# Gate and up projections of a SwiGLU block with tokens on partitions: half-size products of 512 moving columns, turned for the down projection

## The chip, the core and the metric

The kernel runs on one core of one Trainium2 chip. A core has five engines with a queue each: TensorE (PE; its weight loads are listed as PEld), VectorE (DVE), ScalarE (ACT), GpSimd (POOL) and SyncE (SP, which here issues the loads and stores). The metric is the device time of one execution in microseconds, as a median over several runs. A profiled execution gives, beside its own time, a trace of every instruction; the span is the time from its first to its last instruction.

## The reference

One decoder block on 512 tokens of width 1024, all float32. Two token mixers (retention and forgetting attention) are merged and projected, and a gated feed-forward follows, which is what the change touches:

```python
h2 = rmsnorm(x, g_ffn[l])
ff = (jax.nn.silu(h2 @ w_gate[l]) * (h2 @ w_up[l])) @ w_down[l]
x = x + ff
```

`x` is (512, 1024), `w_gate` and `w_up` are (1024, 2816), `w_down` is (2816, 1024). The norm is one factor per token (`rstd`) and one weight per column (`g_ffn`).

## The kernel before

**Numbers in two parts.** Every float32 operand of a large product is split into a high part in the type float32r (a cast on ACT) and a low part, the difference (a subtraction on DVE). Each 128-deep step of a product is then three matmuls: high by high, and the two mixed ones (`three`). A weight therefore costs a load, a cast on ACT and a subtraction on DVE before PE can use it.

**Half-size products.** A product of two matrices cut into 2x2 blocks is formed from seven block products instead of eight, with sums of blocks on both sides (Strassen's scheme in Winograd's form). The sums of x are called S1 to S4, the sums of weights T1 to T4. `xfh` and `xfl` hold the parts of x, feature-major, one pair of tiles for each of four pairs of column blocks j, in slots A11, A21, A12, A22, S1, S2, S3 of 256 tokens; S4 takes A21's slot when that is no longer needed. x carries `g_ffn` already; the factor per token, `r2`, is applied to the results. It is `rstd2` spread over all partitions: `broadcast_cols` copies it wide, turns it on PE and copies it back.

**Gate and up.** Results lie with features on partitions, in `pf`, 22 tiles of 128 features by 512 tokens. The first 256 features of gate and of up are whole products of 512 moving columns (`whole_products`, 48 matmuls each). The other ten blocks of 256 features, gate and up in turn, are half-size products (`half_products`): the weight block is the stationary operand, x the moving one, with 256 tokens per matmul, 7 products x 4 steps x 3 = 84 matmuls. Their weights come one block ahead through `factors`: one load of 1 MB, three DVE operations of sums and three pairs of cast and low part, in tiles of 1024 and 1536 columns. `quarters` adds the pieces up on DVE, then the gate is multiplied by r2 and goes through silu, and up is multiplied in.

**Down.** The last 14 of the 22 tiles of `pf` go through whole products (`prepare` loads and splits a row block of `w_down` and splits pf's tile; eight accumulators, one for each 128 output columns, fill all eight banks of PSUM; tiles `hl` hold pf's parts). During that stage `p_sums` makes the sums for the first eight tiles, which go through half-size products with weights from `factors` and end in the store.

**Order.** PE's order is the program's wherever `pinned` is set. On DVE and ACT a scheduler orders the instructions when the program is built, except where `after(a, b)` puts a behind b. `queue(ins)` does that for DVE: each instruction given to it comes behind the one given before. The first stages of the kernel (values and gate of the retention, "v/g stage" below) already hold tokens on partitions and use `queue`, for instance with `sum_half` (L407) and `split_raw` (L154, L155). Tiles of one tag share a place in memory; a new tile waits until the old one has been read. Names in the trace leave out the number of a buffer, and every matmul is recorded at L72, every turn (a 128x128 transpose against the identity matrix) at L75.

Of the kernel before, what the change touches and what calls it, by code (L numbers as in the profile page):

```python
# [17 lines left out]
P = 128  # L18
D = 1024
# [34 lines left out]
def block_kernel(ctx: ExitStack, tc, x, xT, c_early, c_tab, c_late, w_qf, w_tok, w_vg, w_a, w_y, w_o, w_gu, w_dn, w_dh, out):  # L54
# [812 lines left out]
    r2 = xp.tile([P, S], F32, name="r2")  # L867
# [45 lines left out]

    B12, B11, B21, B22 = range(4)
    wpools = [wq]
    WT = {"raw": (4, F32), "t13": (2, F32), "t24": (2, F32), "ah": (3, F32R), "al": (3, F32R),
# [3 lines left out]
    def wtile(tag):  # L920
        n, dt = WT[tag]
        two = tag in ("raw", "ah", "al") and len(wpools) > 1
        i = seen.get(tag, 0)
        seen[tag] = i + 1
        return wpools[i % 2 if two else 0].tile([P, n, 512], dt, name=tag, tag=tag)
# [22 lines left out]
    def blocks_of(src, n):  # L948

        raws = [wtile("raw")] if n == 0 else [wtile("t13"), wtile("t24")]  # L950
        for v, raw in enumerate(raws):
            nc.sync.dma_start(out=raw, in_=src if n == 0 else src[:, 2 * v:2 * v + 2, :])
        h, l, ah, al = (wtile(t) for t in (f"ch{n}", f"cl{n}", "ah", "al"))
        cuts = ((raws[0], slice(0, 1), h, l, slice(0, 1)),)
        cuts += ((raws[0], slice(1, 4), ah, al, slice(0, 3)),) if n == 0 else ((raws[0], slice(1, 2), ah, al, slice(0, 1)), (raws[1], slice(0, 2), ah, al, slice(1, 3)))
        for raw, a, hh, ll, b in cuts:
            blocks_of.last = nc.scalar.copy(out=hh[:, b, :], in_=raw[:, a, :]), tt(out=ll[:, b, :], in0=raw[:, a, :], in1=f32(hh)[:, b, :], op=ALU.subtract)
        return {"B12": ((h, l), 0), "B11": ((ah, al), 0), "B21": ((ah, al), 1), "B22": ((ah, al), 2)}

    def whole_products(w, ks, step):  # L960
        accs = [bank("acc") for _ in range(2)]
        for n, k in enumerate(ks):
            j, odd = k // 2, k % 2
            mh, ml = (f[j][:, 2 * odd:2 * odd + 2, :].rearrange("p s t -> p (s t)") for f in (xfh, xfl))
            for m2 in range(2):
                (h, l), i = w[f"B{odd + 1}{m2 + 1}"]
                fs = slice(j * P, (j + 1) * P)
                three(accs[m2], h[:, i, fs], l[:, i, fs], mh, ml, n == 0, n == NK - 1)
            step(n)
        return accs  # L970

# [8 lines left out]
    def half_products(w, q, casts=None):  # L980

        x, y, z = (bank(t)[:, 0:HT] for t in ("sc", "acc", "acc"))
        u = fp.tile([P, 4, HT], F32, name="u", tag="u", bufs=2)
# [20 lines left out]


    ws = [blocks_of(w_gu[0, 0], 0)]
    x_sums(3)
    tmp.release()
    mgp.release()
    wp.release()  # L1010
    fp = tc.alloc_tile_pool(name="fp", bufs=1, side="left")
    fp.tile([P, 64], F32, name="pad")
    wpools += [fp]
    pf = fp.tile([P, NF, S], F32, name="pf")
    r2b = r2.rearrange("p (o t) -> p o t", o=1).broadcast_to([P, 2, S])
    rstd2 = rstd1
    EVEN_FIRST = (0, 2, 4, 6, 1, 3, 5, 7)

    def beside_gate(n):
        if n == 6:  # L1020
            pb = bank("tp")
            for t in range(NT):
                mm(pb[:, t:t + 1], lhsT=sqs[:, t * P:(t + 1) * P], rhs=ones[:, 0:1], start=True, stop=True)
            rsqrt(rstd2, pb[:, 0:NT], 1.0 / D, [P, NT], "n1", behind=blocks_of.last[1])

    def beside_up(n):
        if n == 6:
            broadcast_cols(rstd2, r2, fp.tile([P, 4, HT], F32, name="d", tag="d")[:, 0:2, :].rearrange("p a (b t) -> p (a b) t", t=P))
            for m2 in range(2):
                tt(out=pf[:, m2, :], in0=gate[m2], in1=r2, op=ALU.mult)  # L1030
# [231 lines left out]
```

## Time and profile before

| what | value |
|---|---|
| median of 3 runs | 707.72 us (707.56 to 708.82) |
| the profiled execution | 709.25 us, its span 707.5 us |
| granted TensorE clock, mean | 0.999 |
| PE busy | 701.2 us (99% of the span) |
| DVE busy | 535.5 us (76%) |
| ACT busy | 362.0 us (51%) |
| first gate matmul to first matmul of the whole down products | 360.87 to 587.62 us, 226.75 us |
| whole down products | 587.62 to 663.80 us, 76.18 us |
| half-size down products and the end | 663.80 to 707.50 us, 43.70 us |

The profiled execution lies 1.5 us above the median. In the lines shown below, a row of a timeline gives start, length, engine, line of the program, operation, output <- inputs, shapes, and, in brackets, the engine's idle time before it with what ended it. A row of the groups gives the count, the busy time and the mean ns of one. A recorded matmul is longer than the distance to the next, since matmuls overlap; the pace is read from the starts.

### The profile page before, as it was taken

What the parts mean: (1) busy time and instruction counts of PE and PEld (TensorE: products, weight loads), DVE (VectorE), ACT (ScalarE), POOL (GpSimd) and SP (SyncE); (2) the same over time, 40 slices, a digit from 0 to 9 for tenths busy, and PEclk for the clock granted to TensorE, in tenths of its full rate; (3) what the DMA queues carried; (4) which work ended last, traced back from release to release, by engine and by line L of the source; (5) the groups of instructions that cost most, each with busy time, mean ns of one, the idle gap of its engine ahead of it and who ended that gap; (6) DMA issues with size and microseconds to landing.
All of it is one profiled execution on the core that took longest, in us unless ns stands there. A gap on an engine that the chain in (4) does not pass through costs nothing.

```text
span 707.5 us, 10876 instructions
## 1 busy us (share of the span) xinstructions
PE 701.2 (99%) x4283; PEld 619.2 (88%) x4283; DVE 535.5 (76%) x873; ACT 362.0 (51%) x558; POOL 71.6 (10%) x90
## 2 busy tenths in 40 slices
PE   8999999999999999999999999999999999999998
PEld 6888988888877768888888999999999998888998
DVE  6799477754788765748867989898988997844694
ACT  6677453232667566326544755565566555433251
POOL 0004941201122110000220000000000000000000
PEclk9999999999999999999999999999999999999999
DMA  7901312223432312239212322332233114343112
GB/s 280 419 20 31 120 60 90 75 84 99 132 106 91 103 61 65 93 111 327 89 32 88 121 87 93 120 120 71 110 120 120 60 61 134 117 166 113 51 62 74
DMA packets 20547, 77.37 MB, mean 109 GB/s; under 512 B 2440, under 2 KB 3080, under 8 KB 17296
## 3 DMA queue, kind: packets, MB, share of 16 engines
q1 hardware_dynamic: 20352, 76.67, 32.1%
q8 instruction: 33, 0.54, 0.3%
q14 instruction: 18, 0.15, 0.1%
q10 hardware_dynamic: 144, 0.02, 0.0%
HBM read 73.52 MB, written 2.11 MB: 107 GB/s over the span
## 4 chain that ended last, share of the span: by engine, by line
PE 95%; DVE 2%; DMA 1%; issue 1%; ACT 1%; POOL 0%; SPq 0%; DVEq 0%; POOLq 0%
PE acc L72 60%; PE sc L72 28%; PE tp L72 5%; PE tp L75 2%; DMA raw<-in_w_tok_dram 1%; POOL cb L680 0%; DMA cb<-cd 0%; DVE tq L667 0%; DVE pr L688 0%; DVE sg L737 0%; ACT tk L659 0%; DVE pr L692 0%; ACT pr L690 0%; ACT wh L154 0%; DVE ri L691 0%
## 5 line engine op out<-in xcount | busy, mean ns | idle before, releaser
L154 ACT CAST wh<-raw 128x1024 fp32r<-128x1024 f32 (+1 forms) x44 | 46.1, 1049 | 83.4 <-PE acc L72 79.4
L72 PE MATMUL sc<-xfh,cl 128*128 128x256 f32 x288 | 83.2, 289 | 0.0
L72 PE MATMUL sc<-xfh,ch 128*128 128x256 f32 x288 | 81.6, 283 | 0.0
L72 PE MATMUL sc<-xfl,ch 128*128 128x256 f32 x288 | 81.4, 283 | 0.0
L155 DVE TENSOR_TENSOR wl<-raw,wh 128x1024 fp32r<-128x1024 f32 (+1 forms) x44 | 57.0, 1296 | 17.7 <-ACT wh L154 17.5
L929 DVE TENSOR_TENSOR cl<-t,ch 128x1024 fp32r<-128x1024 f32 x48 | 58.6, 1222 | 13.7 <-ACT ch L929 13.6
L72 PE MATMUL acc<-xfh,ah 128*128 128x256 f32 (+1 forms) x216 | 63.9, 296 | 0.0
L72 PE MATMUL acc<-xfh,al 128*128 128x256 f32 (+1 forms) x216 | 63.7, 295 | 0.0
L72 PE MATMUL acc<-xfl,ah 128*128 128x256 f32 (+1 forms) x216 | 63.7, 295 | 0.0
L929 ACT CAST ch<-t 128x1024 fp32r<-128x1024 f32 x48 | 50.5, 1052 | 12.8 <-PE tp L72 8.0
L72 PEld LDWEIGHTS sc<-xfh,cl 128*128 128x128 f32 x288 | 55.0, 191 | 0.8 <-DVE cl L929 0.2
L72 PEld LDWEIGHTS sc<-xfh,ch 128*128 128x128 f32 x288 | 55.1, 191 | 0.2
L72 PEld LDWEIGHTS sc<-xfl,ch 128*128 128x128 f32 x288 | 55.1, 191 | 0.0
L72 PE MATMUL acc<-xh,wh 128*128 128x512 f32 x128 | 53.2, 416 | 0.0
L72 PE MATMUL acc<-wh,xh 128*128 128x512 f32 (+2 forms) x144 | 50.4, 350 | 0.0
L72 PE MATMUL acc<-xh,wl 128*128 128x512 f32 x128 | 50.2, 392 | 0.0
L72 PE MATMUL acc<-xl,wh 128*128 128x512 f32 x128 | 50.0, 391 | 0.0
L72 PE MATMUL acc<-wh,xl 128*128 128x512 f32 (+2 forms) x144 | 49.4, 343 | 0.0
L72 PE MATMUL acc<-wl,xh 128*128 128x512 f32 (+2 forms) x144 | 49.3, 342 | 0.0
L929 DVE TENSOR_TENSOR al<-raw,ah 128x1536 fp32r<-128x1536 f32 x24 | 42.2, 1756 | 6.9 <-ACT ah L929 6.9
L72 PEld LDWEIGHTS acc<-xfh,al 128*128 128x128 f32 x216 | 41.3, 191 | 1.0
L72 PEld LDWEIGHTS acc<-xfl,ah 128*128 128x128 f32 x216 | 41.3, 191 | 0.9
(322 smaller groups left out, 1903.2 us busy)
## 6 DMA issues: line engine op xcount, KB each, us to landing
raw<-in_w_gu_dram SPq DMA_DIRECT2D x21, 1024.0 KB, 4.8
raw<-in_w_a_dram SPq DMA_DIRECT2D x16, 512.0 KB, 3.6
t<-in_w_dn_dram SPq DMA_DIRECT2D x14, 512.0 KB, 3.6
blk<-in_w_vg_dram SPq DMA_DIRECT2D x8, 512.0 KB, 10.0
raw<-in_w_tok_dram SPq DMA_DIRECT2D x8, 512.0 KB, 3.6
raw<-in_w_y_dram SPq DMA_DIRECT2D x8, 512.0 KB, 3.6
raw<-in_w_o_dram SPq DMA_DIRECT2D x8, 512.0 KB, 3.9
raw<-in_w_dh_dram SPq DMA_DIRECT2D x4, 1024.0 KB, 5.0
```

What stands on the lines that cost most here:

```text
L72: in_order(nc.tensor.matmul(o, **kw))
L75: in_order(nc.tensor.transpose(out=o, in_=src, identity=ident))
L154: split_raw.last = (nc.scalar.copy(out=h[:, :width], in_=raw[:, :width]), tt(out=l[:, :width], in0=raw[:, :width], in1=f32(h)[:, :width], ...
L155: tt(out=l[:, :width], in0=raw[:, :width], in1=f32(h)[:, :width], op=ALU.subtract))
L929: split_to.last = nc.scalar.copy(out=h, in_=src), tt(out=l, in0=src, in1=f32(h), op=ALU.subtract)
```

## The change

Gate and up are computed with tokens on partitions. Now x is the stationary operand and the weights move, and the 2x2 blocks of the weights are no longer halves of one matrix: the two column halves are gate and up. The 2816 features go in six groups, five of 512 and one of 256 (`GROUPS`); in each group a block product has 4 steps (j) x 2 halves of 128 tokens (tp) x 3 matmuls of 512 (256) moving columns, seven of them (`gu`): A12, A11, S1, S2, S3, S4, A22, in this order.

A group's weights come as eight loads of 512 KB (`load_group`), into tiles of their own. The sums of weights are made in place (`sum_of`), half a block at a time (two of the four j), and each half is split by `part` into one of three places (`ring_parts`). Every sum and every low part goes through `queue`, in the order written.

Results are collected in `us` (two tiles, one for each tp), copied from PSUM by ACT (`keep`) and added up on DVE through `queue`. The factor per token is now a scalar per partition, so it goes into silu's scale and into the final multiplication; r2, its broadcast and the multiplications by it are gone. `put_h` turns the result on PE, four 128x128 transposes for each of 22 chunks of 128 features, and ACT copies each chunk into `pf`. For group g this happens during group g + 1, and for the last group behind the first matmuls of the down stage.

The whole down products keep their count; their tiles lie in other places, their first matmuls are reordered, and `prepare` and `p_sums` no longer multiply by r2. The pool `wq` is released behind them, and a new pool `wd` holds the tiles of the half-size down products in its place; `factors` for the first of these is called behind the whole products instead of ahead of the last of them.

```diff
-def block_kernel(ctx: ExitStack, tc, x, xT, ..., w_o, w_gu, w_dn, w_dh, out):
+def block_kernel(ctx: ExitStack, tc, x, xT, ..., w_o, w_gu, w_gl, w_dn, w_dh, out):
...
+    GROUPS = [512] * 5 + [256]
+    ring, fq = [0], None
+    def load_group(g, which):
+        w = GROUPS[g]
+        for b in which:
+            if b == B21 and g % 2:
+                halves_ = fq.tile([P, 2, 1024], F32, name="b21", tag="b21")
+                halves_ = [halves_[:, v, :] for v in range(2)]
+            else:
+                halves_ = [wq.tile([P, 1024], F32, name=f"b{b}{v}", tag=f"b{b}{v}") for v in range(2)]
+            for v in range(2):
+                nc.sync.dma_start(out=halves_[v][:, :2 * w], in_=w_gu[g, b, v] if w == 512 else w_gl[b, v])
+            raws[g][b] = [f[:, :2 * w] for f in halves_]
+    def ring_parts():
+        i = ring[0] % 3
+        ring[0] += 1
+        if i < 2:
+            return [wq.tile([P, 1024], F32R, name=n, tag=f"{n}{i}") for n in ("ph", "pl")]
+        hl = fq.tile([P, 2, 1024], F32R, name="hl", tag="hl")
+        return [hl[:, v, :] for v in range(2)]
+    def part(raw, pinned_=True):
+        w2 = raw.shape[-1]
+        h, l = (f[:, :w2] for f in ring_parts())
+        nc.scalar.copy(out=h, in_=raw)
+        low = tt(out=l, in0=raw, in1=f32(h), op=ALU.subtract)
+        if pinned_:
+            queue(low)
+        else:
+            turn_of[0] = low
+        return h, l
+    def sum_of(g, b, c, v):
+        queue(tt(out=raws[g][b][v], in0=raws[g][b][v], in1=raws[g][c][v], op=ALU.add))
+        return raws[g][b][v]
+    def gu(os, parts, slot, new, w, by_bank=False, middle=None):
+        steps = [(j, tp) for j in range(4) for tp in range(2)]
+        for i, (j, tp) in enumerate(sorted(steps, key=lambda s: s[1]) if by_bank else steps):
+            if i == 4 and middle:
+                middle()
+            h, l = parts[j // 2]
+            cs = slice(j % 2 * w, j % 2 * w + w)
+            sh, sl = (f[j][:, slot, tp * P:(tp + 1) * P] for f in (xfh, xfl))
+            for n, (a, b) in enumerate(((sh, h), (sl, h), (sh, l))):
+                mm(os[tp][:, :w], lhsT=a, rhs=b[:, cs], start=new and j + n == 0, stop=j == 3 and n == 2, skip_group_check=not new)
+    HALF = 8
+    parts_of = {}
+    def prepare(k):
+        n = k - HALF
+        raw = wq.tile([P, 1024], F32, name="raw", tag=("b00", "b01", "b30", "b31")[n % 4])
+        nc.sync.dma_start(out=raw, in_=w_dn[n])
+        h, l = ring_parts()
+        cast = nc.scalar.copy(out=h, in_=raw)
+        if n > 0:
+            after(cast, prepare.last)
+        tt(out=l, in0=raw, in1=f32(h), op=ALU.subtract)
+        if n % 4 == 0:
+            hl = xp.tile([P, 2, S], F32R, name="hl", tag="s4")
+        elif n % 4 == 3:
+            hl = fq.tile([P, 2, S], F32R, name="hl", tag="b21")
+        else:
+            hl = wq.tile([P, 2, S], F32R, name="hl", tag=f"b2{n % 4 - 1}")
+        ph, pl = hl[:, 0, :], hl[:, 1, :]
+        prepare.last = nc.scalar.copy(out=ph, in_=pf[:, k, :])
+        if n > 0:
+            after(prepare.last, cast)
+        tt(out=pl, in0=pf[:, k, :], in1=f32(ph), op=ALU.subtract)
+        parts_of[k] = (h, l, ph, pl)
...
+    raws = [[None] * 4 for _ in GROUPS]
+    load_group(0, (B11, B12, B21, B22))
+    ahead = {0: [part(raws[0][B11][0], False), part(raws[0][B11][1])]}
+    for v in range(2):
+        sum_of(0, B11, B12, v)
+    x_sums(3)
+    tmp.release()
+    mgp.release()
+    wp.release()
+    fq = tc.alloc_tile_pool(name="fq", bufs=1, side="left")
+    fq.tile([P, 64], F32, name="pad")
+    second = [part(raws[0][B21][v]) for v in range(2)]
+    rstd2 = rstd1
+    fp = None
+    hs = {}
+    def put_h(g, cs):
+        for c in cs:
+            pb = bank("tp")
+            for t in range(NT):
+                turn(pb[:, t * P:(t + 1) * P], hs[g][t][:, c * P:(c + 1) * P])
+            nc.scalar.copy(out=pf[:, 4 * g + c, :], in_=pb)
+    pinned[0] = True
+    for g, w in enumerate(GROUPS):
+        us = [fq.tile([P, 4, 512], F32, name=f"us{tp}", tag=f"us{tp}") for tp in range(2)]
+        us = [f[:, :, :w] for f in us]
+        x_, z_, y_ = [bank("acc") for _ in range(2)], [bank("acc") for _ in range(2)], [bank("sc") for _ in range(2)]
+        def keep(slot, os):
+            for tp in range(2):
+                nc.scalar.copy(out=us[tp][:, slot, :], in_=os[tp][:, :w])
+        if g == 0:
+            gu(x_, ahead[0], A11, True, w)
+            keep(0, x_)
+            gu(y_, second, A12, True, w)
+            parts = [part(raws[0][B11][v]) for v in range(2)]
+            for j in range(4):
+                split_x(j, S4, s4[:, j, :])
+            fp = tc.alloc_tile_pool(name="fp", bufs=1, side="left")
+            pf = fp.tile([P, NF, S], F32, name="pf")
+        else:
+            gu(y_, ahead[g], A12, True, w)
+            put_h(g - 1, (0, 1))
+            second = [ahead[g, 1], part(raws[g][B11][1])]
+            gu(x_, second, A11, True, w, middle=lambda: put_h(g - 1, (2, 3)))
+            keep(0, x_)
+            parts = [part(sum_of(g, B11, B12, v)) for v in range(2)]
+        if g + 1 < len(GROUPS):
+            load_group(g + 1, (B21,))
+        gu(z_, parts, S1, True, w)
+        keep(3, z_)
+        if g == 0:
+            pb = bank("tp")
+            for t in range(NT):
+                mm(pb[:, t:t + 1], lhsT=sqs[:, t * P:(t + 1) * P], rhs=ones[:, 0:1], start=True, stop=True)
+        parts = [part(sum_of(g, B11, B22, v)) for v in range(2)]
+        gu(x_, parts, S2, False, w)
+        keep(1, x_)
+        if g == 0:
+            turn_of[0] = rsqrt(rstd2, pb[:, 0:NT], 1.0 / D, [P, NT], "n1", behind=turn_of[0])
+        for tp in range(2):
+            queue(tt(out=us[tp][:, 0, :], in0=y_[tp][:, :w], in1=us[tp][:, 0, :], op=ALU.add))
+            act(out=us[tp][:, 0, :], in_=us[tp][:, 0, :], func=AF.Silu, scale=rstd2[:, tp:tp + 1])
+        parts = [part(sum_of(g, B12, B22, v)) for v in range(2)]
+        if g + 1 < len(GROUPS):
+            load_group(g + 1, (B12,))
+        gu(x_, parts, S3, False, w)
+        keep(2, x_)
+        parts = [part(raws[g][B22][v]) for v in range(2)]
+        if g + 1 < len(GROUPS):
+            load_group(g + 1, (B22,))
+        gu(z_, parts, S4, False, w)
+        parts = [part(sum_of(g, B11, B21, v)) for v in range(2)]
+        if g + 1 < len(GROUPS):
+            load_group(g + 1, (B11,))
+        for tp in range(2):
+            queue(tt(out=us[tp][:, 3, :], in0=us[tp][:, 3, :], in1=us[tp][:, 2, :], op=ALU.subtract))
+        if g + 1 < len(GROUPS):
+            ahead[g + 1] = [part(raws[g + 1][B21][0])]
+        gu(x_, parts, A22, False, w, by_bank=True)
+        for tp in range(2):
+            queue(tt(out=us[tp][:, 1, :], in0=z_[tp][:, :w], in1=us[tp][:, 1, :], op=ALU.subtract))
+        for tp in range(2):
+            queue(stt(out=us[tp][:, 0, :], in0=us[tp][:, 1, :], scalar=rstd2[:, tp:tp + 1], in1=us[tp][:, 0, :], op0=ALU.mult, op1=ALU.mult))
+        if g + 1 < len(GROUPS):
+            ahead[g + 1].append(part(raws[g + 1][B21][1]))
+        else:
+            prepare(HALF)
+        for tp in range(2):
+            act(out=us[tp][:, 2, :], in_=x_[tp][:, :w], func=AF.Silu, scale=rstd2[:, tp + 2:tp + 3])
+            queue(stt(out=us[tp][:, 2, :], in0=us[tp][:, 3, :], scalar=rstd2[:, tp + 2:tp + 3], in1=us[tp][:, 2, :], op0=ALU.mult, op1=ALU.mult))
+            if tp == 0 and g + 1 < len(GROUPS):
+                ahead[g + 1, 1] = part(raws[g + 1][B11][0])
+        hs[g] = [us[0][:, 0, :], us[1][:, 0, :], us[0][:, 2, :], us[1][:, 2, :]]
+    pinned[0] = False
+
+    accs = [bank(("sc", "acc", "acc", "tp")[b // 2]) for b in range(8)]
+    x1q = x1.rearrange("p (g a) (s t) -> p g (a s) t", a=2, s=2)
+    pinned[0] = True
+    def whole(k, ms):
+        h, l, ph, pl = parts_of[k]
+        for m in ms:
+            fs = slice(m * P, (m + 1) * P)
+            three(accs[m], h[:, fs], l[:, fs], ph, pl, k == HALF, k == NF - 1)
+            if k == NF - 1:
+                tt(out=x1[:, m, :], in0=accs[m], in1=x1[:, m, :], op=ALU.add)
+    whole(HALF, (0, 1, 4, 5, 2, 3))
+    put_h(len(GROUPS) - 1, (0, 1))
+    prepare(HALF + 1)
+    whole(HALF + 1, (0, 1, 4, 5, 2, 3))
+    whole(HALF, (6, 7))
+    whole(HALF + 1, (6, 7))
+    for k in range(HALF + 2, NF):
+        prepare(k)
+        if (k - HALF) % 3 == 2 and k // 3 - 3 < 4:
+            p_sums(k // 3 - 3)
+        whole(k, range(NK))
+    wq.release()
+    wd = tc.alloc_tile_pool(name="wd", bufs=1, side="right")
+    WT = {"raw": (4, F32, "us0"), "ah": (3, F32R, "b21"), "al": (3, F32R, "hl"), "t13": (2, F32), "t24": (2, F32),
...
-    def whole_products(w, ks, step):
...
-    r2b = r2.rearrange("p (o t) -> p o t", o=1).broadcast_to([P, 2, S])
...
-    for n in range(2, NF):
-        f2, g = n // 2, n % 2
-        if n < NF - 1:
-            ws.append(factors(w_gu[(n + 1) % 2, (n + 1) // 2]))
-        else:
-            prepare(HALF)
-        pp = pf[:, 2 * f2:2 * f2 + 2, :]
-        qq = pp.rearrange("p a (s t) -> p (a s) t", s=2)
-        q = qq if g == 0 else fp.tile([P, 4, HT], F32, name="d", tag="d")
-        done = half_products(ws[n], q, factors.casts if n < NF - 1 else None)
-        if n == 2:
-            after(factors.casts[0], half_products.early)
-            for m2 in range(2):
-                after(act(out=pf[:, m2, :], in_=pf[:, m2, :], func=AF.Silu), half_products.early)
-                tt(out=pf[:, m2, :], in0=up[m2], in1=pf[:, m2, :], op=ALU.mult)
-        quarters(q, *done)
-        if g == 0:
-            tt(out=pp, in0=pp, in1=r2b, op=ALU.mult)
-            act(out=pp, in_=pp, func=AF.Silu)
-        else:
-            tt(out=qq, in0=qq, in1=q, op=ALU.mult)
...
-    for k in range(HALF, NF):
-        if k > HALF:
-            prepare(k)
-        if (k - HALF) % 3 == 2 and k // 3 - 3 < 4:
-            p_sums(k // 3 - 3)
-        if k == NF - 1:
-            ws = [factors(w_dh[0])]
-        h, l, ph, pl = parts[k]
...
+    u2 = fq.tile([P, 2, 4, HT], F32, name="u2", tag="us1")
+    def u_tile():
+        turns_u[0] += 1
+        return u2[:, turns_u[0] % 2]
+    turns_u = [0]
+    ws = [factors(w_dh[0])]
```

More of the change, by code (lines that the diff above doesn't have):

```diff
@@ L53, in block_kernel @@
 @with_exitstack
[L54 removed]
+def block_kernel(ctx: ExitStack, tc, x, xT, c_early, c_tab, c_late, w_qf, w_tok, w_vg, w_a, w_y, w_o, w_gu, w_gl, w_dn, w_dh, out):
     nc = tc.nc
@@ L1026, in beside_up @@
[L1026 to L1030, printed above, removed]
-        if n < 4:
-            split_x(n, S4, s4[:, n, :])
-    pinned[0] = True
-    ws.append(blocks_of(w_gu[1, 0], 1))
-    gate = whole_products(ws[0], (0, 2, 4, 1, 3, 5, 6, 7), beside_gate)
-    seen["raw"] = 2
```

115 lines of the change are left out of this document (23 added, 92 removed).

## The prediction

> **What bounds the kernel now.** I read the page first: total, busy engines, clock, chain of waits, DMA issues.
>
> ```profile
> span 707.5 us, 10876 instructions
> PE 701.2 (99%) x4283; PEld 619.2 (88%) x4283; DVE 535.5 (76%) x873; ACT 362.0 (51%) x558; POOL 71.6 (10%) x90
> PEclk9999999999999999999999999999999999999999
> PE 95%; DVE 2%; DMA 1%; issue 1%; ACT 1%; POOL 0%; SPq 0%; DVEq 0%; POOLq 0%
> t<-in_w_dn_dram SPq DMA_DIRECT2D x14, 512.0 KB, 3.6
> raw<-in_w_dh_dram SPq DMA_DIRECT2D x4, 1024.0 KB, 5.0
> ```
>
> TensorE (PE) holds 95% of the chain at full clock. Second, the table by stage, cut at the first gate matmul, the first of the whole down products, and the first half-size down product.
>
> ```profile
> core 0: us, PE busy (x) PEld busy (x) DVE busy (x) ACT busy (x) POOL busy (x), PEclk, DMA share, GB/s
> 360.87:587.62 226.75, 226.73 (x1790) 221.98 (x1789) 200.11 (x257) 125.67 (x188) 2.64 (x2) 1.00 0.28 96
> 587.62:663.80 76.18, 76.18 (x338) 63.06 (x338) 50.21 (x57) 31.15 (x35) 0.00 (x0) 1.00 0.37 118
> 663.80:707.50 43.70, 40.55 (x337) 40.24 (x335) 29.51 (x40) 15.16 (x24) 0.00 (x0) 0.99 0.20 73
> ```
>
> Gate and up last 226.75 with PE never idle; VectorE (DVE) is second at 200, ScalarE (ACT) at 126. Third, the chain in order of time (start, length, what).
>
> ```profile
> 30.13 16.32 PE acc L72 x72
> ...
> 403.05 2.88 PE sc L72 x24
> 405.93 1.44 PE acc L72 x12
> ...
> 413.21 2.88 PE sc L72 x24
> ```
>
> 72 matmuls of 512 columns in 16.32: 0.2267 each. 12 of 256 columns in 1.44: 0.1200. A block of 256 features (84 matmuls) recurs every 413.21 - 403.05 = 10.16, so 512 features of gate and up cost 40.6.
>
> **The change: PE.** Before: 1680 matmuls of 256 columns and 96 of 512. After: five groups of 168 with 512 columns (38.1 each) and one of 168 with 256 (20.2): 210.6. Added are 88 turns of 128x128. From the timeline of PE:
>
> ```profile
> 74.52 0.60 PE L75 MATMUL tp<-ctab,wide 128*128 128x128 f32 x4
> 74.96 0.60 PE L75 MATMUL tp<-ctab,rot 128*128 128x128 f32 x4
> 75.32 0.36 PE L72 MATMUL acc<-wh,xh 128*128 128x256 f32 x1
> 75.52 0.28 PE L72 MATMUL acc<-wl,xh 128*128 128x256 f32 x1
> ```
>
> Eight turns take 75.32 - 74.52 = 0.80, and the matmul behind them 0.20 instead of 0.12: 0.88 a pair of chunks. Ten of the eleven pairs fall in this stage (8.8), one in the down stage (0.9). With the 0.8 of the column sums of squares, which stay, PE needs 210.6 + 8.8 + 0.8 = 220.2 against 226.75: 6.5 less; 5.6 with the eleventh pair. The removed broadcast of r2 is inside the 226.75.
>
> The Trainium skill speaks against this gain: "TensorE: Matmul & The Clock Gate", section "Back-to-back issue gap", gives columns / 2.4 + 2.5 ns per matmul. By it a merged pair saves 2.5 ns, not the 13.3 of the rows; 840 pairs give 2.1, the 6144 fewer columns 2.6, and the turns would eat both: an estimate of some 231 for PE alone. The rows are of this kernel's own matmuls, so they decide.
>
> **VectorE's chain.** A weight half (two of the four column pairs, 128x1024) must be cast to its high part by ACT, and DVE must subtract that to get the low part; for S1, S2, S3 and A22 DVE first adds two blocks. New is that `queue` strings DVE in the order written: sum 0, low 0, sum 1, low 1. The low part waits for ACT's cast, the cast for that sum, and DVE, which takes its queue in order, stands still meanwhile; behind it stand the next sum and, through that, the next product. The same pattern runs in this kernel's v/g stage. DVE there:
>
> ```profile
> 36.91 1.23 DVE L407 TENSOR_TENSOR blk<-blk,blk 128x1024 f32<-128x1024 f32 x1
> ...
> 40.45 0.16 DVE L115 TENSOR_SCALAR n1v<-ss 128x4 f32<-128x4 f32 x1
> ...
> 42.74 1.23 DVE L155 TENSOR_TENSOR wl<-blk,wh 128x1024 fp32r<-128x1024 f32 x1
> ...
> 47.37 1.22 DVE L407 TENSOR_TENSOR blk<-blk,blk 128x1024 f32<-128x1024 f32 x1
> 48.51 1.22 DVE L419 TENSOR_TENSOR sl<-sums,sh 128x1024 fp32r<-128x1024 f32 x1
> 49.76 1.23 DVE L155 TENSOR_TENSOR wl<-blk,wh 128x1024 fp32r<-128x1024 f32 x1
> 50.91 1.22 DVE L407 TENSOR_TENSOR blk<-blk,blk 128x1024 f32<-128x1024 f32 x1
> ...
> 62.56 1.28 DVE L460 TENSOR_TENSOR vr<-sc,u 128x512 f32<-128x512 f32 x2
> 63.76 1.61 DVE L155 TENSOR_TENSOR wl<-raw,wh 128x1024 fp32r<-128x1024 f32 x1
> ```
>
> and ACT beside it:
>
> ```profile
> 38.22 1.06 ACT L154 CAST wh<-blk 128x1024 fp32r<-128x1024 f32 x1 [0.69 <-DVE blk L407]
> 40.37 0.59 ACT L429 COPY u<-acc 128x512 f32<-128x512 f32 x1 [1.09 <-PE acc L72]
> 40.87 1.05 ACT L154 CAST wh<-blk 128x1024 fp32r<-128x1024 f32 x1
> ...
> 48.68 1.06 ACT L154 CAST wh<-blk 128x1024 fp32r<-128x1024 f32 x1 [0.57 <-DVE blk L407]
> ```
>
> Sum at 47.37, cast from 48.68 to 49.74, low part at 49.76, next sum at 50.91: one link is 3.54, and so is 36.91 to 40.45. In the v/g stage another operation fills the wait (48.51); in the new loop none stands between. A half on PE is 12 x 0.2267 = 2.72, so a product made of sums is fed slower than it is eaten. Per group of 512, eight halves are sums, six are not (low part 1.14, from 49.76 to 50.91), and ten operations of 512 elements take 0.60 each (two from 62.56 to 63.76): 8 x 3.54 + 6 x 1.14 + 10 x 0.60 = 41.2. That exceeds PE's 38.1 + 1.76 = 39.8: DVE's chain becomes the bound, idle ten us of each 41 while it sets the pace.
>
> Where it shows: call 0 the start of product A12. B11's second half can be cast only when its place in the ring of three is read (2.7 + 0.2), and with what DVE still owes the last group the first sum of S1 starts near 5.5. Six links (21.2), the two additions to us0 (1.2) and some 0.3 for ACT copies ahead of a cast bring S3's last low part to 28.2 to 28.6. PE wants it after 5.4 + 0.9 + 5.4 + 0.9 + 5.4 + 5.4 + 2.7 + 0.45 = 26.6. So S3 stalls about 1.9, and a group takes 41.7. Behind S3 the chain recovers: S4's halves need no sum, and A22 goes bank by bank, so its second half is wanted only after a quarter of the product. Were S3's delay gone, the 41.2 of the chain would still bind, and the wait would come up at A22 or at the next S1. A ring place that is freed late shifts the same wait about and adds little to it.
>
> The first group needs no S1 sums on the way, but `rsqrt` stands in the chain (40.45 to 42.74, 2.3): PE 38.9, late 2.6, so 41.5. For the last, half as wide, durations by form, DVE and then ACT:
>
> ```profile
> L943 DVE TENSOR_TENSOR t<-t,raw 128x512 f32<-128x512 f32 x19 | 13.1, 688 | 0.4
> L1003 DVE TENSOR_TENSOR d<-u 128x256 f32<-128x256 f32 x10 | 4.2, 425 | 6.6 <-ACT u L993 6.6
> ```
>
> ```profile
> L929 ACT CAST ch<-t 128x1024 fp32r<-128x1024 f32 x38 | 40.0, 1053 | 1.5 <-issue 1.5
> L1091 ACT ACTIVATE pf<-pf 128x512 f32<-128x512 f32 x2 | 1.2, 626 | 0.0
> L1059 ACT CAST hl<-pf 128x512 fp32r<-128x512 f32 x1 | 0.6, 620 | 1.0 <-DVE pf L1058 1.0
> L252 ACT COPY r<-tp 128x512 f32<-128x512 f32 x1 | 0.6, 587 | 3.4 <-PE tp L75 3.4
> ```
>
> A link is 0.69 + 0.62 + 0.60 + 0.08 = 1.99; 8 x 1.99 + 4 x 0.60 + 10 x 0.37 = 22.0, as much as PE (20.2 + 1.8); with a stall at S3 as above, 23.5. Stage: 41.5 + 4 x 41.7 + 23.5 = 231.8, **5.0 more** than 226.75.
>
> What I cost at nothing: ACT's 14 casts, 8 copies, 4 silu and 4 copies of turned chunks (14.7 + 4.7 + 2.5 + 2.3 = 24 per 41), hidden as long as none stands ahead of a cast (rival B). The loads: 4 MB a group as before, in 512 KB pieces; B11's next half is asked for behind A22's sum and lands 3.6 later, under A22's 5.4; uncovered it would cost up to 3.6 a group. SP's queue only holds loads. GpSimd has nothing here. The start: the fourth column pair of x is first wanted 4.1 after 360.87, and its low part is there:
>
> ```profile
> 361.87 0.75 DVE L902 SCALAR_TENSOR_TENSOR xfl<-x,ce,xfh 128x512 fp32r<-128x512 f32 x1
> ```
>
> In the down stage `prepare` loses its multiplication by r2 and `p_sums` gains splits: DVE has 26 free of 76.
>
> **Two seams.** First, k = 8: its weights take the ring place that S4 of the last group frees 2.9 before PE needs them; cast 1.05, two low parts 1.9, among six short DVE operations. Between 0.3 and 2.5; I take 1.4, since the short ones (0.4 each) may come ahead. The accumulators wait for nothing longer: the first four columns of output use banks that are read early. Second, the half-size down products. Before, their first weights came early:
>
> ```profile
> 647.30 1.48 ACT L929 CAST ah<-raw 128x1536 fp32r<-128x1536 f32 x1 [3.87 <-PE tp L72]
> ```
>
> ```profile
> 648.81 1.76 DVE L929 TENSOR_TENSOR al<-raw,ah 128x1536 fp32r<-128x1536 f32 x1 [2.71 <-ACT ah L929]
> ```
>
> that is 16 ahead of 663.80. Now pool `wd` lies where `wq` lay, and k = 21 reads wq's ring and b20 to its last matmul. If `ah` falls on these, cast and low part follow the end: 1.5 + 1.8 + 0.2 = 3.5. Nothing if it falls elsewhere; 8.2 if even the load (5.0) must wait. I take 2.5.
>
> Sum: 5.0 + 0.9 + 1.4 + 2.5 = 9.8 on the span of 707.5. That execution took 709.25, 1.5 above the median 707.72 of the runs, so I add the difference to the median: **717.5**.
>
> **Rivals.**
> A, faster: the chain does not bind and the seams are hidden: 707.72 - 5.6 = 702.1. A link would have to be under (39.8 - 6.8 - 6.0) / 8 = 3.37; the two links seen are 3.54, so the margin is only 5%. For it the Trainium skill, "Perfetto Trace Analysis", section "Identifying the Most-Contended Engine", judges TensorE by the busy share of weight loads: it is 98% here, and the change drops two loads in five. The trace disagrees that loads set the pace: at 83% (63.06 of 76.18) a matmul still pays the same 13 ns.
> B, much slower: on ACT a PSUM copy (`keep`) is queued ahead of the next product's cast, as at 40.37, where a copy waited 1.09 for PE with a cast behind it. The cast then follows the product's end: 0.2 + 1.1 + 1.05 + 1.22 - 0.45 = 3.1 of PE wait. One such place a group gives five times 3, near 732.5; four would pass 770.
> C, a wash: links as seen, but lateness only just over and the seams hidden, within 0.2% (1.4 us, about what a measurement of this kernel tells from no change).
>
> **Numbers.** DVE's chain with its seams 0.59 (711 to 724: stage 2 to 9 over, as a link takes 3.44 to 3.65 and copies cost up to one more us a group, and the seams' own ends), B 0.16, A 0.16, C 0.09. Slower is the first and B, 0.75; same 0.09; faster 0.16. The range 704 to 733 leaves out the better half of A and the part of B with more than one such place a group, together about 0.18.
>
> **What would show it.** After: some 41.7 between the A12 starts of groups; DVE idle behind ACT casts, about 1.1 at each low part of a sum; PE waiting at S3 for DVE; pairs of turns at 0.88; PE idle near 2.5 before the first half-size down product. Wrong if PE runs through the groups at 39.8 (A), if ACT's idle time before `keep` copies is ended by PE with casts behind (B), or if 512-column matmuls come at another pace than 0.2267.

## The result: slower, by twice what was forecast

The changed kernel takes 729.92 us (median of 4 runs, 729.45 to 732.05) against 708.27 of the kernel before in the same session (4 runs, 707.56 to 708.89): a ratio of 1.0312, 95% interval 1.0288 to 1.0336. The forecast was 717.5.

### The profile after

From the page of the changed kernel: the span, TensorE's share, the granted clock by slices and the chain that ended last.

```profile
span 728.3 us, 9535 instructions
PE 707.4 (97%) x3599; PEld 587.7 (81%) x3599; DVE 520.0 (71%) x845; ACT 373.0 (51%) x570; POOL 72.2 (10%) x90
...
PEclk9999999999999999999999999999999999999799
...
PE 80%; DVE 9%; ACT 6%; issue 3%; DMA 2%; POOL 1%; ACTq 0%; SPq 0%; DVEq 0%; POOLq 0%
```

TensorE is busy for longer than before (707.4 against 701.2) although it has less to do. Part of its waiting is counted as busy: a matmul that comes behind a wait is recorded longer (0.50 instead of 0.39 at 428.30), and the four middle groups show 163.94 busy where a later version, in which TensorE does not stand still, needs 159.60. The chain shows it better: TensorE holds 80% of it, before 95%. The clock drops in one slice, from 674 to 692 us.

The table by stage, cut at the starts of the first group, the second group, the last group, the whole down products and the half-size down products (columns as in the table of before):

```profile
360.74:404.39 43.65, 41.30 (x177) 33.12 (x176) 34.82 (x48) 26.45 (x35) 3.16 (x2) 0.96 0.37 121
404.39:570.80 166.41, 163.94 (x738) 131.83 (x738) 128.44 (x131) 93.19 (x122) 0.00 (x0) 1.00 0.26 83
570.80:596.74 25.94, 23.69 (x188) 22.23 (x186) 19.74 (x37) 17.29 (x34) 0.00 (x0) 1.00 0.24 82
596.74:673.63 76.89, 76.88 (x342) 63.43 (x342) 43.56 (x65) 28.02 (x42) 0.00 (x0) 1.00 0.27 83
673.63:728.30 54.67, 43.43 (x336) 42.63 (x336) 34.92 (x44) 17.60 (x26) 0.00 (x0) 0.90 0.28 97
```

Gate and up take 236.0 (43.65 + 166.41 + 25.94) instead of 226.75, 9.25 more. The whole down products take 0.7 more. The last stage takes 54.67 instead of 43.70, 11.0 more. Together that is the 20.8 by which the span grew, with 0.1 less ahead of them. There are two losses, and the larger one is not in the stage that was changed most.

The groups, in the chain in order of time (start, length, what): the first product A12 of the second, the third and the last group, and a pair of turns.

```profile
404.39 5.44 PE sc L72 x24
...
446.02 5.44 PE sc L72 x24
451.46 0.87 PE tp L75 x8
...
570.80 2.87 PE sc L72 x24
```

The first distance is 41.63, the four together 166.41, 41.60 each (none is further than 0.04 from it), where 41.7 was forecast. In the waits of these four groups (total, times, longest) the rows say what the casts on ScalarE wait for:

```profile
DVE pl L942 <- ACT ph L941: 25.4, 21, 1.4
ACT ph L941 <- DVE b L950: 16.7, 14, 2.5
...
DVE hl L942 <- ACT hl L941: 12.5, 11, 1.4
ACT hl L941 <- DVE b L950: 8.3, 9, 2.5
...
ACT ph L941 <- PE acc L72: 6.1, 9, 2.5
...
PE acc L72 <- ACT us L1033: 1.7, 7, 0.3
...
PE acc L72 <- DVE pl L942: 0.5, 1, 0.5
```

VectorE waits 37.9 for casts, 9.5 a group. The casts wait 25.0 for VectorE's sums (L950), and about half as long, 12.4, for TensorE to free a place (6.1 in the row shown; three smaller rows, two of them for `hl`, make up the rest). So VectorE and ScalarE hold each other up. TensorE itself stands in S3 alone, and there it waits for two things: for a low part, and for ScalarE to copy S2 out of the bank that S3 goes on in (`keep`, L1033). In the chain two of the four groups come out of S3 behind a low part (TensorE goes on at 474.18 and 515.74) and two behind such a copy (429.73 and 554.52). The link on VectorE, sum to sum:

```profile
425.40 1.22 DVE L950 TENSOR_TENSOR b<-b,b 128x1024 f32<-128x1024 f32 x1
...
428.94 1.22 DVE L950 TENSOR_TENSOR b<-b,b 128x1024 f32<-128x1024 f32 x1
```

From 425.40 to 428.94 is 3.54: the link that was read from the v/g stage.

The seam ahead of the half-size down products, in the chain:

```profile
673.65 4.81 DMA raw<-in_w_dh_dram
...
678.55 1.24 DVE t L1150
...
679.81 0.69 DVE t L1155
...
682.23 2.51 PE sc L72 x10
```

and in the timeline of all engines:

```profile
664.29 1.76 DVE L1141 TENSOR_TENSOR al<-raw,ah 128x1536 fp32r<-128x1536 f32 x1 [4.27 <-ACT ah L1141]
...
680.08 0.58 PE L72 MATMUL sc<-xfh,ah 128*128 128x256 f32 x1 [6.47 <-ACT ah L1141]
...
682.23 0.58 PE L72 MATMUL sc<-xfh,al 128*128 128x256 f32 x1 [1.35 <-DVE al L1141]
```

Even the load of the first block starts only as the last whole down product ends (673.63), and the chain goes straight from TensorE's last matmul to it. Yet low parts had been made at 664.29: those of the second block, whose tiles lie in `fq`, a pool that is still alive. The first block is the later one, because its tiles lie in the pool `wd`, which is opened where `wq` was.

### The profile page after: what moved, and what is told of

Same layout as the page of the kernel before. It is cut to its first block, busy times and chain, and to the rows that moved or that the text cites. A ratio compares the mean times of both kernels' runs of the same rounds, so it can differ in the third digit from the quotient of the medians.

```text
span 728.3 us, 9535 instructions
## 1 busy us (share of the span) xinstructions
PE 707.4 (97%) x3599; PEld 587.7 (81%) x3599; DVE 520.0 (71%) x845; ACT 373.0 (51%) x570; POOL 72.2 (10%) x90
## 4 chain that ended last, share of the span: by engine, by line
PE 80%; DVE 9%; ACT 6%; issue 3%; DMA 2%; POOL 1%; ACTq 0%; SPq 0%; DVEq 0%; POOLq 0%
PE acc L72 57%; PE sc L72 15%; PE tp L72 5%; PE tp L75 3%; ACT ph L941 3%; DVE b L950 2%; DVE pl L942 2%; DVE us L1065 1%; ACT hl L941 1%; DMA raw<-in_w_dh_dram 1%; ACT us L1033 1%; DMA raw<-in_w_tok_dram 0%; POOL cb L680 0%; DMA cb<-cd 0%; DVE tq L667 0%
## 5 line engine op out<-in xcount | busy, mean ns | idle before, releaser
L942 DVE TENSOR_TENSOR pl<-b,ph 128x1024 fp32r<-128x1024 f32 (+1 forms) x56 | 63.3, 1138 | 36.2 <-ACT ph L941 36.2
L72 PE MATMUL acc<-ph,xfh 128*128 128x512 f32 (+1 forms) x196 | 74.3, 379 | 2.3 <-ACT us L1033 1.3
L72 PE MATMUL acc<-pl,xfh 128*128 128x512 f32 (+1 forms) x196 | 73.7, 376 | 1.1 <-DVE pl L942 0.9
L941 ACT CAST ph<-b 128x1024 fp32r<-128x1024 f32 (+1 forms) x56 | 54.8, 983 | 38.1 <-DVE b L950 27.8
L72 PE MATMUL acc<-ph,xfl 128*128 128x512 f32 (+1 forms) x196 | 72.9, 372 | 0.0
L72 PE MATMUL acc<-hl,xfh 128*128 128x512 f32 (+1 forms) x184 | 59.7, 384 | 3.1 <-ACT hl L941 2.3
L950 DVE TENSOR_TENSOR b<-b,b 128x1024 f32<-128x1024 f32 (+1 forms) x48 | 54.2, 1130 | 0.1
L72 PEld LDWEIGHTS acc<-ph,xfh 128*128 128x128 f32 x196 | 36.9, 188 | 10.4 <-ACT us L1033 3.2
L72 PEld LDWEIGHTS acc<-pl,xfh 128*128 128x128 f32 x196 | 36.9, 188 | 10.0 <-DVE pl L942 3.7
L72 PEld LDWEIGHTS acc<-ph,xfl 128*128 128x128 f32 x196 | 36.9, 188 | 6.1
L941 ACT CAST hl<-b 128x1024 fp32r<-128x1024 f32 (+1 forms) x28 | 27.3, 976 | 20.8 <-DVE b L950 9.8
```

Source lines behind the costliest of these rows:

```text
L72: in_order(nc.tensor.matmul(o, **kw))
L941: nc.scalar.copy(out=h, in_=raw)
L942: low = tt(out=l, in0=raw, in1=f32(h), op=ALU.subtract)
L950: queue(tt(out=raws[g][b][v], in0=raws[g][b][v], in1=raws[g][c][v], op=ALU.add))
```

## The experiments

Each kernel is the changed one with the edit shown. The times of before in their sessions are 709.42 (sums first, live pool, first block outside, clock kept), 707.84 (sums and seam, S2 and S3 bank by bank, all of it, no turns) and 709.11 (bank order without sums). They differ by up to 1.6, so a difference to a kernel of another session, such as the 729.92 of the changed one, is sure only to about that much.

### Both sums ahead of both low parts

```diff
-            parts = [part(sum_of(g, B11, B12, v)) for v in range(2)]
+            parts = [part(h) for h in [sum_of(g, B11, B12, v) for v in range(2)]]
 ... and so for S2, S3 and A22
```

> Only the order on VectorE changes: for S1, S2, S3 and A22 both sums of a product come ahead of both low parts, so that the second sum runs while ScalarE casts the first. If the serial link sum-cast-low sets the pace of a group (as the prediction says), DVE's chain falls from 41 to about 8 x 2.28 + 6 x 1.14 + 10 x 0.60 = 31 per group, PE becomes the bound, and the distance between the A12 starts falls from 41.6 to 39.8 plus what PE waits for the copies of S2 out of the bank that S3 goes on with (0.3 to 0.7): 40.1 to 40.5. With the first and the last group (1 to 2.5 each) the time falls by 6.5 to 10, to 720 to 723.5. If the ring of three places or ScalarE's own queue sets the pace, the distance stays above 41.2 and the time within 2 of 729.9.

Measured: 721.05, ratio 1.0172 (1.0155 to 1.0188), 8.9 less than the changed kernel. Starts of A12 in the second, third and last group, in the chain:

```profile
402.10 5.44 PE sc L72 x24
...
443.05 5.44 PE sc L72 x24
...
565.48 2.87 PE sc L72 x24
```

The first distance is 40.95, the four together 163.38, 40.85 each (40.2 to 41.2), a little above the 40.1 to 40.5 expected. The instructions are the same; their order alone gives 8.2 of the 9.25 lost in gate and up back (in the profiled executions): 2.3 in the first group, 2.9 in the last and 3.0 in the four between. Those four still take 163.38, where TensorE alone was priced at 4 x 39.8 = 159.2. The waits of the same four groups:

```profile
DVE pl L942 <- ACT ph L941: 20.2, 22, 2.5
ACT ph L941 <- PE acc L72: 19.0, 19, 2.2
...
DVE hl L942 <- ACT hl L941: 13.0, 13, 2.7
...
PE acc L72 <- ACT us L1033: 1.7, 3, 0.8
```

VectorE still waits 33.2 for casts, but the casts into `ph` now wait for TensorE (19.0, was 6.1) and hardly for sums any more (0.5, was 16.7). VectorE's idle time by itself would not have told the two kernels apart; what the cast waits for does. What is left on TensorE is a wait that the prediction overlooked, as long as in the changed kernel (1.7): S3 accumulates in the same bank as S2, and must wait until ScalarE's `keep(1, x_)` has copied it out (L1033).

### The first block's large tiles in the living pool

```diff
-    seen = {}
+    seen = {"raw": 1, "ah": 1, "al": 1}
```

> Only the places of the first half-size down block change: its load and the parts of its three raw blocks (ah, al) lie in pool fq, which lives on, and the second block's in the new pool wd; the sums t13, t24 and their parts stay in wd. If a tile of the new pool waits until the whole released pool wq has been read, the load comes early and the first product starts within 0.3 of the last whole product, but the sum t13 still starts only at that end: sum 1.2, cast 1.05, low part 1.2 less the 1.4 of the first product leave 2 to 3 of wait, and the clock stays full. Last stage (from the last whole matmul to the end) 54.7 to 46.5 to 48.5; time 721.5 to 724. If only the overlap of single tiles counts, t13 and t24 run before that end, and the stage comes to 43.7 to 45; time 719 to 720.5.

Measured: 722.64, ratio 1.02 (1.0177 to 1.0224), 7.3 less. The timeline at the seam:

```profile
664.64 1.76 DVE L1141 TENSOR_TENSOR al<-raw,ah 128x1536 fp32r<-128x1536 f32 x1 [4.27 <-ACT ah L1141]
...
674.61 1.22 DVE L1150 TENSOR_TENSOR t<-raw 128x1024 f32<-128x1024 f32 x1
```

`raw` had been there since before 664.64, and still the sum `t`, which goes into the new pool, was made at 674.61, behind the last whole product (673.97). So the load is not the whole of the wait. This row alone does not separate the pool from VectorE's order, because `t` also stands right behind the last additions to x1; the next run does. The profiled execution (725.27) is the longest of the four. Its last stage took 49.5, above the 46.5 to 48.5 expected, at a granted clock of 0.92.

### All but one tile of the first block outside the new pool

```diff
+        if i == 0 and tag in EARLY:
+            return EARLY[tag]
...
+    EARLY = {"raw": pf[:, 0:4, :], "t13": pf[:, 4:6, :], "t24": pf[:, 6:8, :], "ch0": c_first[:, 0:2, :], "cl0": c_first[:, 2:4, :],
+             "ch1": xp.tile([P, 2, 512], F32R, name="c1", tag="s4")}
```

`c_first` is a tile in place of `us0`, and `ah` and `al` take `b21` and `hl` of `fq`.

> All tiles of the first half-size down block but one low part (cl1) lie outside the new pool, in places that are free by then (the first eight tiles of pf, us0, b21, hl, s4). If the new pool's wait for the old one is the whole of the seam, the last stage falls from 54.7 to 43.7 to 45, as before the change, with no slow clock behind it: time 718.8 to 720.5, 9.5 to 11 below the changed kernel. If the additions to x1 or the queue of loads hold the first product, PE stays idle over 1.5 there and the stage stays above 46.

Measured: 719.47, ratio 1.0148 (1.0132 to 1.0164), 10.5 less. The last stage in the table by stage:

```profile
673.20:717.60 44.40, 40.73 (x336) 40.25 (x335) 30.80 (x40) 15.72 (x24) 0.00 (x0) 1.00 0.33 119
```

44.40, where before it was 43.70 and after 54.67: the seam's loss is all but gone. The groups stand where they stood. The sum that waited until 674.61 is now written into `pf`, and VectorE makes it 40 us ahead of the last whole product's end (673.19):

```profile
633.00 1.23 DVE L1152 TENSOR_TENSOR pf<-pf 128x1024 f32<-128x1024 f32 x1
```

So it was the place of the tile, and not VectorE's work, that held it. The one low part left in the new pool, cl1, is made at 673.84.

### The clock kept up through the seam

```diff
+    fill_bank = bank("tp")
+    for i in range(28):
+        mm(fill_bank, lhsT=xfh[0][:, 0, 0:P], rhs=xfh[0][:, 0:2, :].rearrange("p s t -> p (s t)"), start=True, stop=True)
```

> The changed kernel with 28 matmuls of 512 columns on any data (6.3 us, their result unused) put behind the last whole product, so that PE is busy while it waits for the first half-size weights. The wait itself stays (weights at the same time). If the slow matmuls behind the seam (0.21 for 256 columns against 0.12) come from the idle time, they run at 0.12 at once, the granted clock of the last stage rises from 0.90 to above 0.97, and the time falls by 1.5 to 3, to 727 to 728.5. If the slow pace has another cause, time and pace stay.

Measured: 729.2, ratio 1.0282 (1.0264 to 1.0301), 0.7 less by the medians and by the profiled spans: a miss. The clock stayed up (1.00 in the last stage, and 0.12 a matmul), but the weights still came when they came:

```profile
682.56 0.38 PE L72 MATMUL sc<-xfh,al 128*128 128x256 f32 x1 [1.64 <-DVE al L1141]
...
686.70 0.39 PE L72 MATMUL sc<-xfh,cl 128*128 128x256 f32 x1 [0.76 <-DVE cl L1141]
```

A faster TensorE only waits longer for `cl` (0.76 instead of 0.23). At this seam the slow clock is a consequence that costs 0.7, not a cause.

### Sums first and the block outside together

> The two edits of e1 (both sums ahead of both low parts) and e3 (first half-size down block outside the new pool) together. They act in different stages, so if they are independent the time is 729.9 - 8.9 - 10.5 = 710.5 (709.5 to 711.5). If the earlier down stage finds its loads or parts late, it ends above 712.

Measured: 712.76 (710.93 to 714.16), ratio 1.0068 (1.005 to 1.0086). The sum of the two edits would be 710.6, so 2.1 is missing, and the time lies above the 712 that the expectation named as the sign of a late part. In the profiled spans the gains add up: 8.2 and 10.7 alone, 19.2 together (709.1 against 728.3). But that execution, 710.93, is the shortest of the four; the longer ones show a lower mean clock (0.997 in that of 714.16, 1.000 in the profiled one), and where they lose it no profile shows. So the two losses are separate in the execution that was profiled, and not fully by the medians.

### And S2 and S3 bank by bank

To the kernel with both edits:

```diff
-        gu(x_, parts, S2, False, w)
+        gu(x_, parts, S2, False, w, by_bank=True)
 ... and so for S3
```

> e5 with S2 and S3 bank by bank, the additions to us0 where they were. If PE's wait for the copies of S2 is the whole of the rest, the distances of the A12 starts become 39.8 to 40.1 and the time falls by 3 to 4 to 706.5 to 708; if the order on VectorE ahead of S3 is part of it, the distances stay at 40.4 or more.

Measured: 708.65 (10 runs, 707.04 to 709.88), ratio 1.0009 (0.9999 to 1.0019), 4.1 less than without. The chain in order of time:

```profile
401.93 5.44 PE sc L72 x24
...
411.87 29.97 PE acc L72 x132
441.83 5.44 PE sc L72 x24
```

A group now takes 39.90 and TensorE does not stand still in it; the forecast's price for TensorE alone was 39.8. The time lies 0.6 above the range expected. The wait for ScalarE's copies of S2 is covered, because the bank that is wanted first is also finished first.

### The bank order without the sums' order

The block outside and `by_bank` for S2 and S3, with sum, cast and low part one after another as in the changed kernel:

> The first block's tiles stand outside the new pool, and S2 and S3 go bank by bank, but each half's sum, cast and low part still follow one another (the links of 3.54 us). With both orders changed the groups came 39.90 apart, with the sums' order alone 40.2 to 41.2, with neither 41.6. Theory (VectorE's chain of sum, cast and low part is a bound of its own, 41.2 a group by its links, whatever the banks do): the A12 starts stay 41.1 to 41.6 apart, time 717.5 to 719.5, and TensorE waits for VectorE's low parts instead of for the copies of ScalarE. Rival (the chain is only near the bound, and what set 41.6 was the accumulator's turnaround between S2 and S3): 39.9 to 40.5 apart, time 711 to 715.

Measured: 739.1, ratio 1.0437 (1.0413 to 1.046): 19.6 more than with the block outside alone (719.47), which neither theory had. The same edit that gave 4.1 with the sums first costs 19.6 without. The four groups, from A12 to A12, and their waits:

```profile
406.85:587.10 180.25, 168.24 (x738) 132.02 (x738) 128.84 (x131) 93.40 (x122) 0.00 (x0) 0.99 0.24 76
```

```profile
DVE pl L942 <- ACT ph L941: 34.0, 24, 3.6
...
DVE hl L942 <- ACT hl L941: 16.6, 12, 2.7
...
ACT ph L941 <- PE acc L72: 13.2, 14, 2.7
```

A group takes 45.06, 3.5 more than 41.60. VectorE's work is the same (128.84 against 128.44), its waits for casts are 50.6 instead of 37.9, 3.2 more a group, and the casts into `ph` wait 13.2 for TensorE instead of 6.1. In the code, a product that goes bank by bank wants its second half after a quarter of its matmuls instead of a half, and reads its first half until three quarters are done, so that half's place in the ring is freed later. The trace shows both, in the first of these groups and alike in the others:

```profile
433.74 0.50 PE L72 MATMUL acc<-hl,xfh 128*128 128x512 f32 x1 [1.02 <-ACT hl L941]
```

```profile
438.51 1.22 DVE L942 TENSOR_TENSOR pl<-b,ph 128x1024 fp32r<-128x1024 f32 x1 [2.42 <-ACT ph L941]
```

The first row is S3's second half, wanted before its cast is done. The second is the low part of S4's second half: its cast got its place only when S3 had let go of its first half, VectorE stood 2.42 for it, and the sums of A22 stand behind it. With the sums first VectorE stands about as long at that low part (2.2 to 2.8 in each group), but A22's sums then follow it back to back, and TensorE waits nowhere. Here it waits for casts and low parts alone (11.8 in all) and no longer for copies, as the theory said, but its 41.1 to 41.6 was wrong: the chain is no bound of its own, since it contains waits for TensorE. How much each of the two adds is not shown. The rival, that the bank's turnaround alone set the 41.6, is refuted by the run with the sums first, where the wait for the bank was as long and the groups came 40.85 apart. This run cannot refute it, because its edit moves more than the turnaround.

### All of it, and a version faster than both

To sums first, block outside and bank order: the additions and silu of `us[.][0]` (and in the first group `rsqrt`) are written behind S3's parts instead of ahead of them, and `prepare(HALF)` ahead of A22, its low parts in VectorE's order.

> e5, and three reorderings: S2 and S3 go bank by bank (all of the first 128 tokens, then all of the second), so that ScalarE's copy of S2 out of a bank is done when S3 goes on in it; the additions to us0, with the norm's factors in the first group, come behind S3's parts on VectorE instead of ahead; the weights of k = 8 are split ahead of the last group's final operations. If what is left above 39.8 per group in e1 (distances 40.2 to 41.2) is PE's wait for those copies, the distances become 39.8 to 40.1 and the first group loses its 2.5 of wait at S3: 4 x 0.9 + 2 + 0.7 less than e5, 703.5 to 706, as much under the kernel before as PE's work is less. If ScalarE's queue puts other copies ahead of casts in the new order, the distances stay above 40.5 and the time at 708 or more.

Measured: 706.08 (8 runs, 705.26 to 706.36), ratio 0.9972 (0.9961 to 0.9982): 1.8 faster than the kernel before, 23.8 faster than the change as it stood, and just above the range expected. Its table by stage:

```profile
360.74:400.95 40.21, 39.58 (x176) 31.85 (x175) 34.43 (x48) 26.19 (x34) 3.17 (x2) 1.00 0.39 128
400.95:560.55 159.60, 159.60 (x738) 132.78 (x738) 129.04 (x131) 94.42 (x122) 0.00 (x0) 1.00 0.28 87
560.55:582.71 22.16, 22.11 (x186) 21.79 (x185) 17.72 (x31) 16.05 (x31) 0.00 (x0) 1.00 0.27 96
```

The groups come 39.90 apart, as with the bank order and the sums first alone, so what this version adds lies outside the four. Gate and up now take 222.0, 4.8 less than before; of that, 1.0 goes in the whole down products and 0.7 in the last stage. The medians differ by less than these spans because the profiled execution of before lies 1.5 above its median.

### The turns taken away

The version ahead of this one without the 88 turns. ScalarE copies each chunk unturned, in two pieces instead of one, so this kernel leaves out what the down products need and computes something else:

> e6 without the 88 turns on PE: ScalarE copies the blocks into pf as they lie, not turned, so the down products work on other data. This is the price of the turns where PE is the bound: eleven pairs at 0.88, so 9 to 10 less than e6. If something else than PE is the bound in the groups, the gain is under 6.

Measured: 696.64, ratio 0.9843 (0.9829 to 0.9856), 9.4 less than with them. A12 starts at 402.12 and 440.19 in its chain, 38.07 apart instead of 39.90, 1.83 for two pairs of chunks where the forecast had 1.76. For all eleven pairs it had 8.8 + 0.9 = 9.7, all of it on TensorE's path.

## Why the prediction was half right

By its own terms, on the span; the forecast's excess is 9.8 and the measured one 20.8:

| term | forecast | measured | difference |
|---|---|---|---|
| first group | 41.5 | 43.65 | +2.1 |
| four groups | 4 x 41.7 | 166.41 | -0.4 |
| last group and the seam to k = 8 | 23.5 + 1.4 | 25.94 | +1.0 |
| whole down products | 76.2 + 0.9 | 76.89 | -0.2 |
| half-size down products | 43.7 + 2.5 | 54.67 | +8.5 |

**The failed step is the second seam.** The prediction named the place (pool `wd` where `wq` lay) and the three cases, 0, 3.5 and 8.2, and took 2.5, between the first two. It was the third: "if even the load (5.0) must wait". (By the prediction's own figures that case is 5.0 + 3.5 = 8.5, not 8.2.) It cost 11.0, more than that case's own price, because the sum stopped at the first low part. Behind the load VectorE first makes the sums `t` (1.24 + 0.69 in the chain), so that the matmul that reads `al` came 8.6 after the last whole product. Then the matmuls ran slowly, and TensorE waited again for `cl`: 2.3 more. The prices were known; the choice among them was made without a row. What decides it is stated by the two runs: with the load moved early, the new pool's tiles still waited (674.61), and with nearly all tiles elsewhere the loss was gone. In no run was a tile of the new pool touched before the last whole product ended. Whether the wait is for the whole old pool or for the particular places underneath, no run separates.

**VectorE's chain held in part.** The link (3.54), the group (41.6 against 41.7) and the wait of 9.5 a group were as forecast, and the stall sits at S3. But in two of the four groups what ends that stall is the copy of S2 out of S3's bank, which no term of the prediction has. The runs share out the excess of the four groups over the 159.60 that they take without a stall: of 6.8, the order of sums and low parts gives 3.0, and the bank order on top of it the other 3.8. So the order is a cause, but not the whole one. That 41.7 came out so close is partly luck: the chain and the copy are late at the same place, and only one of them was counted. What the copy alone costs while the chain is late, no run shows. The bank order without the sums first also answers the sentence that a ring place freed late "adds little": there a late place is one of two causes that add 3.5 a group.

**The first group** was forecast 2.6 late. TensorE's timeline there:

```profile
383.28 0.39 PE L72 MATMUL acc<-pl,xfh 128*128 128x512 f32 x1
385.98 0.79 PE L72 MATMUL acc<-hl,xfh 128*128 128x512 f32 x1 [2.31 <-ACT hl L941]
...
387.24 1.22 PE L72 MATMUL acc<-hl,xfh 128*128 128x512 f32 x2
...
390.63 0.39 PE L72 MATMUL acc<-ph,xfh 128*128 128x512 f32 x1
```

and VectorE beside it:

```profile
385.96 1.23 DVE L942 TENSOR_TENSOR hl<-b,hl 128x1024 fp32r<-128x1024 f32 x1 [1.57 <-ACT hl L941]
```

The gap is 385.98 - 383.28 - 0.23 = 2.5, as forecast. Then the 12 matmuls up to 390.63 take 4.65 instead of 2.72: 1.9 more, which was in no term. The third of them, at 387.24, reads the low part that VectorE finishes at 387.19, so 0.8 would be lost at full clock too. The ten from there on take 3.39 instead of 2.27: 1.1 of slow pace. In the version faster than both, with the chain mended and the additions moved, the gap and the slow pace are both gone and the group takes 40.21.

**The rivals.** A (faster, 702.1) needed the chain not to bind and the seams hidden. The chain did bind; once the chain, the bank's turnaround and the seam were mended by hand the kernel came to 706.08, near A's figure but not at it. The estimate of 231 that the prediction sets against TensorE's gain is no rival here. It rests on a formula of the Trainium skill, "TensorE: Matmul & The Clock Gate", section "Back-to-back issue gap", which that section gives for a single isolated matmul. In this trace the 512-column matmuls kept their 0.2267 (24 in 5.44). B's number (732.5) was close to the time measured, but its mechanism was not: where TensorE waited for ScalarE's copies it waited for the bank, not for a cast queued behind them. Where copies do stand ahead of a late cast the price is small: in the first group, with two activations beside them, 0.5 (sum done at 384.39, cast at 384.89), and in the last group 0.1. A number that agrees does not carry its theory along.

## What to carry to other kernels

When two engines alternate on one piece of data (sum here, cast there, difference here again), write all first steps ahead of all last steps, and price the chain by its links rather than by the busy share: VectorE was 77% busy (128.44 of 166.41) and its order alone cost 0.75 a group. Where a pool is opened in the place of one still read, look for the first touch of its tiles in a trace and, as long as there is none, take the full chain (load, sums, cast, low part) as the price; tiles in a pool that lives on avoid it. A reordering that helps one wait should be tried together with the others: here the same line was worth minus 4.1 or plus 19.6.

## What was not expected of the hardware

The clock can fall after a short pause. Behind the gap of 2.5 us at 383.5, ten 512-column matmuls came 0.34 apart on average (3.39 in all, with both parts of their weights ready) instead of 0.2267; after the 6.45 us at the second seam, ten 256-column matmuls took 2.3 (starts from 682.23 to 684.52) instead of the 1.2 of full pace. The stages' granted clocks are 0.96 and 0.90. The Trainium skill, "TensorE: Matmul & The Clock Gate", section "What's actually happening", puts the fall to half speed after an idle window of about 3.4 us; the first of these gaps is shorter than that, so here a gap of 2.5 us must already be priced with a slow stretch behind it. The length of the pause does not settle it alone: with the first block's large tiles in the living pool, the profiled execution has pauses of only 1.6 and 1.0 at the seam, and behind them 256-column matmuls came 0.21 apart up to 684.4 (a clock of 0.92 in its last stage, 0.992 over the whole), while the other three executions of the same kernel show 0.998 and are 2.6 us shorter. What the stretch costs depends on what else is late: 1.1 in the first group, but 0.7 at the seam, where filling the pause with idle matmuls showed that the weights, not the clock, set the time.
